# Spreading decay rows by one two-part product, regrouping the key products, and inverting 32x32 blocks on VectorE alone

## The chip, the cores and the metric

The kernel runs on one core of a Trainium2 chip. The metric is device microseconds of the whole launch, the median of several runs of the same program on the same inputs. Five engines of the core work side by side, each through its own instruction queue in order: TensorE (PE; its weight loads are listed as PEld), VectorE (DVE), ScalarE (ACT), GpSimd (POOL) and SyncE (SP), which here issues every DMA. TensorE's clock is granted at one of two levels, 1.2 or 2.4 GHz; the profile gives the granted share of full speed.

## The reference

Two layers of a backbone over 1024 latent tokens and 256 context tokens (1280 together, ten tiles of 128). A layer normalises and modulates its input, projects it by one wide matrix, gives the columns to four groups of four heads each (mLSTM, differential attention, GLA, gated DeltaNet), and brings the four outputs together in an output projection with a gated residual. In the second layer only the latent tokens are put out.

The change lies in the gated DeltaNet. For each direction, each head and each chunk of 64 tokens the reference has:

```
gc = cumsum(g)                                   # along the chunk
decay[t, s] = exp(gc[t] - gc[s])  for s <= t, else 0
lower = (beta k k^T) * decay, strictly below the diagonal
tmat = (I + lower)^-1                            # unit lower triangular, 64x64
u = tmat (v beta),  w = tmat (k beta exp(gc))
attn = (q k^T) * decay
```

A scan over the chunks uses u, w and attn after that. The second direction reads the tokens from the end.

## The kernel before

Two strands of work share the engines. The left one projects: `Proj.run` multiplies the normalised activations by `w_in` block by block (16 blocks a layer; the tiles `mm` of the profile, in two PSUM banks), and then does the mLSTM. The right one goes through a layer in the order `gates`, `gdn`, `attention`, `gla`, and the output projection runs behind them. Layer 1's projections start as layer 0's output rows come in.

The order of the instructions is not written out by hand. All strands hand their next operation to a planner (class `Issue`, from line 131), which keeps a clock per engine from its own cost formulas and takes the operation that can start first, with ranks between strands (`RANK`, line 34: the projections are last with 4, the decays have 1, most of the DeltaNet 0) and with a preference for dense products where its count of streamed columns runs low. What it picks is emitted at once, so its guesses fix each engine's queue; at run time an engine waits at the head of its queue.

The DeltaNet's part before the scan has these steps in each layer:

- `gates` (from line 891) computes rows over all tokens, among them X1 (log decay sum plus log beta) and NCG (minus the decay sum), 8 rows each (direction by head), and writes each by DMA to a DRAM tile of its own, `rs`.
- `gate_columns` (line 1043) reads 8 such tiles back into `pk` (64 rows by 1280 tokens), and PE transposes it to columns `tokc`.
- `gdn_decays` (line 1412) builds exponents as matrices, "column + row": the row has to stand on 32 or 64 partitions. `by_block`, `by_partner` and `by_chunk` do this on PE: the weights are one column of the identity, spread over 32 or 64 columns, the moving side is `pk`, in float32. `by_block` and `by_partner` issue four products of 64x32 weights and 320 columns each, `by_chunk` two of 64x64. There are 28 such units in a layer (8 + 4 + 16), through two PSUM tiles `e`; in the trace a float32 product is two instructions, so they are 160. DVE adds the columns (one operation a unit), POOL adds the mask (16 operations a layer), ACT takes the exponential. The strands `spread` (PE), `exps` (POOL, ACT) and the main one (DVE) hand units over by events.
- `products` in `gdn_rest` (line 1521) multiplies, per tile of 128 tokens and per head, keys by keys in four 32-blocks (64x32 weights) and keys by queries in two 64-chunks (64x64 weights), into `po` and `p1`. Even heads lie on partitions 0 to 63, odd heads on 64 to 127. DVE multiplies the results with the decays into `LT`, `Lo` and `ats`.
- The inverse of every 32x32 diagonal block is by elimination in 31 steps over `Z`: 96 blocks to a partition group are held as three sets of 32x32 on 128 partitions. `steps` (line 1568) does a step as a product into `ltmp` and a subtraction from `Z`. VectorE does sets 0 and 1, each by instructions of its own, GpSimd set 2, in a strand `on_pool`, which at its end clears `T64` for what follows.
- The 64x64 inverses are put together from the blocks by transposes on DVE and 32x32 products on PE; then the scan begins.

In layer 0 the convolution and normalisation of the DeltaNet's inputs (`gdn_front`) and the modulation products (`mod`) run beside the decays; in layer 1 only `gdn_front`.

Of the kernel before, what the change touches and what calls it, by code (L numbers as in the profile page):

```python
# [39 lines left out]
def _consts():  # L40
    f = np.float32
    c = {}
    c["k_zero"] = np.zeros((1, T), f)
    c["k_ident"] = np.eye(128, dtype=f)
    s = np.arange(128)[:, None]
    t = np.arange(128)[None, :]
    c["k_caus"] = np.stack([np.where(t >= s, 0.0, NEG), np.where(t <= s, 0.0, NEG)], 1).astype(f)
    ls = np.arange(128)[:, None] % 32
    lt = np.arange(32)[None, :]
    c["k_m32"] = np.where(lt > ls, 0.0, NEG).astype(f)  # L50
    l6, t6 = np.arange(128)[:, None] % 64, np.arange(64)[None, :]
    c["k_m64"] = np.stack([np.where(t6 >= l6, 0.0, NEG), np.where(t6 <= l6, 0.0, NEG)], 1).astype(f)
    ls = ls.astype(int)
    c["k_lev"] = np.stack([((ls // (2 << j)) == (lt // (2 << j))) & ((ls >> j) != (lt >> j)) for j in range(5)], 1).astype(f)
    bo = np.zeros((128, 128), f)
    bo[:64, :64] = 1
    bo[64:, 64:] = 1
    c["k_bones"] = bo

    sc = np.ones((64, T + 1), f)  # L60
    for r in range(64):
        sc[r, ::128 if r % 32 < 4 else 64] = 0
    c["k_scan"] = sc
    prm = np.zeros((128, 3), f)
    for d in range(2):
        g = 32 * d
        prm[g:g + 4] = (1, 1, 0)
        prm[g + 4:g + 8] = (-1, 0, -1)
        prm[g + 16:g + 32] = (1, 1, 0)
        g = 64 + 32 * d  # L70
        prm[g:g + 4] = (-1, 0, -1)
        prm[g + 4:g + 8] = (1, 0, -1)
    c["k_prm"] = prm
    rows = NLAT // GRID_W
    row = np.repeat(np.arange(rows), GRID_W).astype(f)
    col = np.tile(np.arange(GRID_W), rows).astype(f)
    half = 16
    inv = np.power(f(10000.0), -np.arange(0, half, 2, dtype=f) / f(half)).astype(f)

    def tab(p):  # L80
        ang = (p[:, None] * inv).astype(f)
        ang = np.concatenate([ang, ang], -1)
        return np.cos(ang).astype(f), np.sin(ang).astype(f)

    cr, sr = tab(row)
    cc, scn = tab(col)
    cos = np.concatenate([cr, cc], -1)
    sin = np.concatenate([sr, scn], -1)
    sgn = np.concatenate([-np.ones(8), np.ones(8)] * 2).astype(f)
    cos_all = np.concatenate([np.ones((NCTX, 32), f), cos], 0)  # L90
    sin_all = np.concatenate([np.zeros((NCTX, 32), f), sin * sgn], 0)
    rp = np.stack([cos_all, sin_all], 1)
    c["k_rope"] = rp.reshape(NT, 128, 2, 32).transpose(1, 0, 2, 3).copy()
    return c
# [325 lines left out]
def _build(tc, nc, A, out, root, dbg):  # L420
# [150 lines left out]
    def dt_(name, shape):  # L571
        return dram(shape, name)
# [15 lines left out]
    dod = [dt_(f"do{l}", [128, NT, 256]) for l in L2]  # L588
    dad = [[dt_(f"da{l}_{t}", [128, 8, 64]) for t in range(NT)] for l in L2]
    QN = ("A", "EM", "WS", "NCG", "X1", "EX1", "EX2", "BH", "NG", "WI", "CG", "EG")  # L590
    rsd = [{q: dt_(f"rs{l}_{q}", [8, T]) for q in QN} for l in L2]
    ald = [dt_(f"al{l}", [128, 2, T]) for l in L2]
    AB = [cst([128, 2, 2, 8], f"AB{l}") for l in L2]

# [696 lines left out]
    def gdn(L):  # L1291
        l = L.l
        mark(f"{l}gdn")
        D = Box()
        with ExitStack() as D.st:
            D.ep = Pool(D.st, "gdn", side="right")
            D.st0 = ExitStack()
            D.gp = Pool(D.st0, "gtri", side="right")
            D.LT = D.gp([128, 96, 32], "LT")
            D.Lo = D.gp([128, 40, 32], "Lo")  # L1300
            D.EB = D.ep([128, 5120], "EB")
            D.st1 = ExitStack()
            kp = Pool(D.st1, "keys", side="right")
            D.K = [kp([128, T], f"K{i}") for i in range(2)]
            with ExitStack() as st2:
                D.pk = Pool(st2, "dec", side="right")([64, T], "pk")
                q_.spawn(RANK["decays"], lambda: gdn_decays(L, D, Pool(st2, "dcps", PSUM, "right")))
                for hp in range(2):
                    q_.need((l, "kq", 0, hp))
                    dma(D.K[hp], featd["dkn"][l][:, hp])  # L1310
                q_.need((l, "dec", "e"))
            q_.need((l, "front"))
            kp = Pool(D.st1, "queries", side="right")
            D.Q = [kp([128, T], f"Q{i}") for i in range(2)]
            for hp in range(2):
                q_.need((l, "kq", 1, hp))
                dma(D.Q[hp], featd["dq"][l][:, hp])
            gdn_rest(L, D)
# [93 lines left out]
    def gdn_decays(L, D, pps):  # L1412
# [3 lines left out]
        l = L.l  # L1416
        mark(f"{l}gdn.dec")
        pk, LT, Lo = D.pk, D.LT, D.Lo
        gate_columns(L, pk)
        rows = pk.rearrange("p (t b i) -> p t b i", b=4, i=32)  # L1420
        rows64 = pk.rearrange("p (t c i) -> p t c i", c=2, i=64)
        E2 = D.EB.rearrange("p (l i) -> p l i", i=64)
        first = LT[:, 80:82, :].rearrange("p a b -> p (a b)")[:, :4 * NT].rearrange("p (t h) -> p t h", h=4)
        ib = 8 * QN.index("NCG")
# [4 lines left out]
        def by_block(q, dh):  # L1429

            ps = pps([128, NT, 32], "e", 2)
            for b in range(4):
                r = 8 * QN.index(q) + dh
                P.matmul(ps[32 * b:32 * b + 32], ident[:64, r:r + 1].to_broadcast([64, 32]), rows[:, :, b, :],
                         start=True, stop=True, tile_position=(0, 32 * b))
            return ps

        def by_partner(q, h):

            ps = pps([128, NT, 32], "e", 2)  # L1440
            for b in range(4):
                r = 8 * QN.index(q) + 4 * (b % 2) + h
                P.matmul(ps[32 * b:32 * b + 32], ident[:64, r:r + 1].to_broadcast([64, 32]), rows[:, :, b ^ 1, :],
                         start=True, stop=True, tile_position=(0, 32 * b))
            return ps

        def by_chunk(q, dh, t0):

            r = 8 * QN.index(q) + dh
            ps = pps([128, 5, 64], "e", 2)  # L1450
            for c in range(2):
                P.matmul(ps[64 * c:64 * c + 64], ident[:64, r:r + 1].to_broadcast([64, 64]), rows64[:, t0:t0 + 5, c, :],
                         start=True, stop=True, tile_position=(0, 64 * c))
            return ps

        def tcol(q, dh, n=32, t0=0, m=NT):
# [48 lines left out]
    def gdn_rest(L, D):  # L1505
# [15 lines left out]
        def products():  # L1521
            for t in range(NT):
                if t > 1:
                    q_.need(ev("done", t - 2))

                pk = pks[t] = [pps([128, 2, 128], f"{('po', 'p1')[t % 2]}{x}") for x in range(2)]
                for h in range(4):
                    hp, x = divmod(h, 2)
                    xs = slice(64 * x, 64 * x + 64)
                    for b in range(4):  # L1530
                        t0 = 128 * t + 32 * b
                        both = K[hp][xs, t0 - 32 * (b % 2):t0 - 32 * (b % 2) + 64].rearrange("p (c i) -> p c i", i=32)
                        P.matmul(pk[x][32 * b:32 * b + 32, hp, 0:64].rearrange("p (c i) -> p c i", i=32), K[hp][xs, t0:t0 + 32],
                                 both[:, ::-1] if b % 2 else both, start=True, stop=True, tile_position=(64 * x, 32 * b))
                    for c in range(2):
                        t0 = 128 * t + 64 * c
                        P.matmul(pk[x][64 * c:64 * c + 64, hp, 64:128], K[hp][xs, t0:t0 + 64], Q[hp][xs, t0:t0 + 64],
                                 start=True, stop=True, tile_position=(64 * x, 64 * c))
                q_.set(ev("pk", t))
# [18 lines left out]
        with ExitStack() as st2:  # L1558
# [6 lines left out]
            for s_ in range(3):  # L1565
                V.transpose(Y[:, s_], LT[:, 32 * s_:32 * s_ + 32, :].rearrange("p l t -> p t l"))

            def steps(E, parts):

                for j in range(31):  # L1570
                    m, n = 31 - j, j + 1
                    tv = {}
                    for s_ in parts:
                        tmp = lp([128, 272], f"ltmp{s_}")
                        tv[s_] = tmp[:, :m * n].rearrange("p (a b) -> p a b", b=n)
                        E.tensor_tensor(tv[s_], Y[:, s_, j + 1:, j:j + 1].to_broadcast([128, m, n]),
                                        Z[:, s_, j:j + 1, 0:n].to_broadcast([128, m, n]), ALU.mult)
                    for s_ in parts:
                        E.tensor_tensor(Z[:, s_, j + 1:, 0:n], Z[:, s_, j + 1:, 0:n], tv[s_], ALU.subtract)

            def on_pool():
                mark(f"{l}gdn.inv")
                steps(G, (2,))
                G.memset(T64, 0.0)
                q_.set((l, "inv"))
            q_.spawn(0, on_pool)
            steps(V, (0, 1))
            q_.need((l, "inv"))

            TT, TN = gp([128, 96, 32], "LT"), lp([128, 3, 32, 32], "Y").rearrange("p a b c -> p (a b) c")  # L1590

# [1324 lines left out]
```

## Time and profile before

| | |
|---|---|
| median of three runs | 2483.91 us (2483.13 to 2484.88) |
| the profiled execution | 2481.02 us |
| its span, first to last instruction | 2479.1 us |
| PE busy | 2194.1 us |
| DVE busy | 1521.1 us |
| ACT busy | 980.7 us |
| POOL busy | 905.9 us |
| mean granted TensorE clock | 0.94 |

The span is what the profile's views divide up; the profiled execution's time lies 1.9 us above its span, and the median 2.9 us above that. Busy times are shares of the span of each engine, and they overlap. Nearly all instructions pass through one helper, so they share one source line (L396), and groups are told apart by tile names: `mm` is the projections, `e` the spread rows, `po` and `p` with `K` the key products, `Z` and `ltmp` the inverse.

### The profile page before, as it was taken

Reading aid. Unit: us, or ns where it says so; the run is one execution under the profiler, and the core shown is the slowest. Engines: PE = TensorE matmul, PEld = TensorE weight load, DVE = VectorE, ACT = ScalarE, POOL = GpSimd, SP = SyncE. Lnnn points to the kernel's source line nnn. Section 1 sums busy time; section 2 is a strip of 40 time slices with the busy share of each in tenths; the row PEclk is TensorE's granted clock in tenths of the full one; section 3 lists DMA queues with packets and bytes.
Section 4 is the critical chain, followed back from the end, with each engine's and each line's share of the span. In section 5 each row is a group of like instructions: output and inputs, shape, how many; then the busy total and the mean of one; then the engine's idle time right before and its main releaser. Section 6 shows DMA issues by size and latency. Waiting matters only on the chain. (4 is left out here: it accounts for less than half of the span.)

```text
span 2479.1 us, 58334 instructions
## 1 busy us (share of the span) xinstructions
PE 2194.1 (89%) x23631; PEld 1772.2 (71%) x23631; DVE 1521.1 (61%) x2786; ACT 980.7 (40%) x2123; POOL 905.9 (37%) x1201
## 2 busy tenths in 40 slices
PE   5899999999988998887877899989899898977989
PEld 2666589888776777775755676888778677765777
DVE  3587449664277773447556486587633587746665
ACT  3346211333266773223334265222332476732240
POOL 2233428363212224422431245373533122255340
PEclk7899999999999999998989999999999999976999
DMA  7446442364423215258963244333343422163595
GB/s 258 123 134 226 155 144 92 104 185 143 131 81 99 71 30 149 72 143 229 267 206 115 68 128 144 127 118 101 119 145 108 126 61 67 48 157 97 153 295 182
DMA packets 343414, 334.61 MB, mean 135 GB/s; under 512 B 88762, under 2 KB 287642, under 8 KB 342634
## 3 DMA queue, kind: packets, MB, share of 16 engines
q1 hardware_dynamic: 343146, 330.88, 44.7%
q8 instruction: 187, 3.06, 0.5%
q14 instruction: 81, 0.66, 0.1%
HBM read 225.98 MB, written 107.43 MB: 134 GB/s over the span
## 5 line engine op out<-in xcount | busy, mean ns | idle before, releaser
L396 PE MATMUL mm<-w,hT 128*128 128x256 f32 x4512 | 635.5, 292 | 16.7 <-ACT st L396 5.8
L396 PEld LDWEIGHTS mm<-w,hT 128*128 128x128 f32 x4512 | 571.1, 193 | 58.3 <-issue 31.4
L396 PE MATMUL mm<-hT,w 128*128 128x512 f32 (+1 forms) x1680 | 389.9, 378 | 13.1 <-ACT hT L396 3.7
L396 PEld LDWEIGHTS mm<-hT,w 128*128 128x128 f32 x1680 | 283.1, 194 | 86.0 <-issue 21.2
L396 DVE TENSOR_REDUCE st<-sc 128x1 f32<-128x1024 f32 (+1 forms) x200 | 200.3, 1026 | 85.8 <-PE sc L396 84.4
L396 ACT ACTIVATE p<-sc,st 128x256 f32<-128x256 f32 (+1 forms) x272 | 211.2, 785 | 74.0 <-DVE st L396 55.4
L396 POOL TENSOR_TENSOR hss<-hss,mhalf 128x2 f32<-128x2 f32 (+2 forms) x72 | 103.3, 1435 | 179.0 <-DVE hss L396 171.1
L396 PE MATMUL o<-wo,yT 128*128 128x512 f32 x540 | 151.3, 420 | 5.1 <-DVE x L396 4.8
L396 PE MATMUL sc<-KT,qt 96*128 96x512 f32 (+1 forms) x400 | 123.7, 399 | 31.0 <-DMA KT<-akh 18.4
L396 POOL TENSOR_TENSOR w<-wr,w 128x512 fp32r<-128x512 f32 x60 | 86.3, 1442 | 158.7 <-ACT w L396 120.7
L396 ACT COPY st<-mm 128x512 f32<-128x512 f32 (+1 forms) x84 | 46.1, 549 | 224.1 <-PE mm L396 182.5
L396 POOL TENSOR_TENSOR ss<-ss,mhalf 128x1 f32<-128x1 f32 (+1 forms) x39 | 67.2, 1723 | 183.8 <-DVE ss L396 172.4
L396 POOL TENSOR_TENSOR st<-st 128x1 f32<-128x1 f32 (+1 forms) x136 | 28.0, 206 | 278.1 <-ACT p L396 202.2
L396 ACT COPY wt<-tr 128x512 f32<-128x512 f32 (+1 forms) x200 | 102.3, 511 | 63.8 <-PE tr L396 63.4
L396 PEld LDWEIGHTS o<-wo,yT 128*128 128x128 f32 x540 | 104.8, 200 | 30.0 <-DVE x L396 4.5
L396 PE MATMUL tr<-k_ident,p 128*128 128x128 f32 x656 | 115.1, 281 | 10.1 <-ACT wt L396 9.8
L396 PE MATMUL o<-w,yT 128*128 128x512 f32 x324 | 103.1, 444 | 20.9 <-DVE st L396 15.1
L396 ACT CAST w<-wr 128x512 fp32r<-128x512 f32 x128 | 76.8, 622 | 92.6 <-DMA wr<-in_w_in 58.4
L396 PEld LDWEIGHTS sc<-KT,qt 96*128 96x128 f32 x400 | 63.5, 195 | 59.3 <-ACT p L396 31.8
L396 PE MATMUL po<-wt,av 128*64 128x128 f32 x1312 | 104.6, 284 | 1.4 <-DVE aacc L396 1.4
L396 DVE SCALAR_TENSOR_TENSOR p<-p,st,p 128x1280 f32<-128x1280 f32 (+1 forms) x72 | 103.0, 1431 | 3.1 <-POOL st L396 3.1
L396 PEld LDWEIGHTS tr<-k_ident,p 128*128 128x128 f32 x656 | 75.8, 141 | 36.6 <-ACT wt L396 21.1
(315 smaller groups left out, 4257.3 us busy)
## 6 DMA issues: line engine op xcount, KB each, us to landing
wr<-in_w_in SPq DMA_DIRECT2D x64, 512.0 KB
wm<-in_w_mod SPq DMA_DIRECT2D x64, 256.0 KB
y<-y SPq DMA_DIRECT2D x36, 256.0 KB
xp<-st SPq DMA_DIRECT2D x18, 512.0 KB
pd<-rs_NG SPq DMA_DIRECT2D x18, 512.0 KB
kq<-kq SPq DMA_DIRECT2D x18, 512.0 KB
x<-xp SPq DMA_DIRECT2D x18, 512.0 KB
wm<-in_w_mod SPq DMA_DIRECT2D x16, 512.0 KB
```

The lines of the kernel that those rows point to most:

```text
L396: r = fn(*a, **k)
```

## The change

Three edits. First, the rows are spread by one float32r product a unit with 128x128 weights in place of two or four float32 products. To that end X1 and NCG lie in one DRAM tile; sixteen DMAs and one of a constant bring them to `stage`, arranged so that the 128 partitions are two copies (`part`) of 4 token blocks by 16 rows; ACT rounds `stage` to float32r (`both`, 784 columns), DVE turns the second copy of the rows into what the rounding left over; a 0/1 weight matrix, which ACT spreads out of a 0/1 column for each unit (`adder`), sums the two. The DMAs are issued ahead of those of `gate_columns`. Second, for each tile all heads' K K products are issued before all heads' K Q products. Third, VectorE does all three sets of a step of the inverse in one instruction, and GpSimd only clears `T64` at the last step.

```diff
-    rsd = [{q: dt_(f"rs{l}_{q}", [8, T]) for q in QN} for l in L2]
+    rsd = [{q: dt_(f"rs{l}_{q}", [8, T]) for q in QN if q not in ("X1", "NCG")} for l in L2]
+    rs2 = [dt_(f"rs{l}_X1_NCG", [16, T]) for l in L2]
+    for l in L2:
+        rsd[l].update(X1=rs2[l][0:8], NCG=rs2[l][8:16])
...
+        stage = D.dp([128, 784], "stage")
+        for part in range(2):
+            for b in range(4):
+                dma(stage[64 * part + 16 * b:64 * part + 16 * b + 16, 0:320].rearrange("p (t i) -> p t i", i=32),
+                    rs2[l].rearrange("r (t b i) -> b r t i", b=4, i=32)[b])
+                c, th = divmod(b, 2)
+                dma(stage[64 * part + 16 * b:64 * part + 16 * b + 16, 320:640].rearrange("p (t i) -> p t i", i=64),
+                    rs2[l].rearrange("r (a t c i) -> c a r t i", a=2, c=2, i=64)[c, th])
+        dma(stage[:, 640:784], A["k_pick"])
         gate_columns(L, pk)
-        rows = pk.rearrange("p (t b i) -> p t b i", b=4, i=32)
-        rows64 = pk.rearrange("p (t c i) -> p t c i", c=2, i=64)
+        both = D.dp([128, T], "pk", dt=F32R)
+        S.copy(both[:, 0:784], stage)
+        V.tensor_tensor(both[64:128, 0:640], stage[64:128, 0:640], both[64:128, 0:640].bitcast(F32), ALU.subtract)
...
+        def adder(pick):
+            i, n = turn[0] % 6, pick.shape[1]
+            turn[0] += 1
+            w = spread_[:, 128 * i:128 * i + 128]
+            S.copy(w.rearrange("p (g i) -> p g i", g=n), pick.bitcast(F32).to_broadcast([128, n, 128 // n]))
+            return w
...
             ps = pps([128, NT, 32], "e", 2)
-            for b in range(4):
-                r = 8 * QN.index(q) + dh
-                P.matmul(ps[32 * b:32 * b + 32], ident[:64, r:r + 1].to_broadcast([64, 32]), rows[:, :, b, :],
-                         start=True, stop=True, tile_position=(0, 32 * b))
+            r = 8 * ("X1", "NCG").index(q) + dh
+            P.matmul(ps, adder(pick_b[:, :, r:r + 1]), blocks, start=True, stop=True)
             return ps
...
                                  both[:, ::-1] if b % 2 else both, start=True, stop=True, tile_position=(64 * x, 32 * b))
+                for h in range(4):
+                    hp, x = divmod(h, 2)
+                    xs = slice(64 * x, 64 * x + 64)
                     for c in range(2):
                         t0 = 128 * t + 64 * c
                         P.matmul(pk[x][64 * c:64 * c + 64, hp, 64:128], K[hp][xs, t0:t0 + 64], Q[hp][xs, t0:t0 + 64],
...
-            q_.spawn(0, on_pool)
-            steps(V, (0, 1))
-            q_.need((l, "inv"))
+            for j in range(31):
+                m, n = 31 - j, j + 1
+                if j == 30:
+                    G.memset(T64, 0.0)
+                tmp = lp([128, 3 * 272], "ltmp")
+                tv = tmp[:, :3 * m * n].rearrange("p (s a b) -> p s a b", s=3, b=n)
+                V.tensor_tensor(tv, Y[:, :, j + 1:, j:j + 1].to_broadcast([128, 3, m, n]),
+                                Z[:, :, j:j + 1, 0:n].to_broadcast([128, 3, m, n]), ALU.mult)
+                V.tensor_tensor(Z[:, :, j + 1:, 0:n], Z[:, :, j + 1:, 0:n], tv, ALU.subtract)
```

`by_partner` and `by_chunk` are changed as `by_block` is. The new constant `k_pick` (128x144) holds the three sets of 0/1 columns.

## Rows read from the trace of the kernel before

**Rows 1.** The page's first part: busy us (share of the span) xinstructions, by engine.
```profile
PE 2194.1 (89%) x23631; PEld 1772.2 (71%) x23631; DVE 1521.1 (61%) x2786; ACT 980.7 (40%) x2123; POOL 905.9 (37%) x1201
```

**Rows 2.** Who waited for whom, PE, 62 to 1057 us: total us, times, longest.
```profile
PE sc L396 <- DMA KT<-akh: 9.6, 2, 5.7
```

**Rows 3.** Chain of waits, end of layer 1: start us, us, what.
```profile
2175.68 11.64 PE mm L396 x96
...
2188.74 8.21 DMA gk<-gqk
```

**Rows 4.** Busy time by stretch: length, engines (xinstructions), PEclk, DMA share, GB/s.
```profile
235.00:306.00 71.00, 68.82 (x467) 35.49 (x467) 34.22 (x53) 22.95 (x39) 28.36 (x28) 0.98 0.46 147
368.00:444.00 76.00, 71.98 (x541) 68.14 (x541) 68.38 (x151) 14.72 (x26) 53.31 (x74) 0.98 0.30 96
1495.00:1566.00 71.00, 67.09 (x483) 46.79 (x482) 49.06 (x52) 34.80 (x53) 42.76 (x35) 0.95 0.32 107
1632.00:1712.00 80.00, 71.57 (x457) 66.38 (x458) 62.22 (x149) 14.52 (x26) 53.95 (x74) 0.91 0.29 94
2170.00:2232.00 62.00, 43.45 (x1056) 40.81 (x1054) 29.69 (x61) 20.06 (x38) 31.53 (x43) 0.76 0.62 156
2232.00:2294.00 62.00, 45.61 (x1510) 36.34 (x1510) 40.31 (x53) 18.73 (x39) 31.71 (x39) 0.69 0.38 96
```

**Rows 5.** The same for the tile `e` alone: PE, PEld, DVE, then the clock.
```profile
235.00:306.00 71.00, 25.20 (x160) 6.34 (x160) 13.29 (x28) 0.98 0.46 147
1495.00:1566.00 71.00, 20.89 (x160) 5.81 (x160) 13.16 (x28) 0.95 0.32 107
```

**Rows 6.** The same for the tile `K` alone, the key products: PE, PEld.
```profile
300.00:357.00 57.00, 21.42 (x480) 13.96 (x480) 1.00 0.46 151
1566.00:1620.00 54.00, 21.77 (x480) 14.31 (x480) 1.00 0.48 157
```

**Rows 7.** Timeline of PE in one tile's key products: start us, us, instructions.
```profile
310.04 0.33 PE L396 MATMUL po<-Q,K 64*64 64x64 f32 x4
310.30 0.32 PE L396 MATMUL po<-K 64*32 64x64 f32 x8
310.55 0.33 PE L396 MATMUL po<-Q,K 64*64 64x64 f32 x4
```

**Rows 8.** Busy time for the tile `Z` alone, the inverse: PE, PEld, DVE, ACT, POOL.
```profile
368.00:444.00 76.00, 0.00 (x0) 0.00 (x0) 52.79 (x123) 0.00 (x0) 37.16 (x62) 0.98 0.30 96
1632.00:1712.00 80.00, 0.00 (x0) 0.00 (x0) 48.02 (x125) 0.00 (x0) 36.18 (x61) 0.91 0.29 94
```

**Rows 9.** Timeline of DVE in layer 0's inverse.
```profile
400.29 1.54 DVE L396 TENSOR_TENSOR ltmp<-Y,Z 128x231 f32<-128x231 f32 x2
...
418.89 0.75 DVE L396 TENSOR_TENSOR ltmp<-Y,Z 128x256 f32<-128x256 f32 x2
419.56 0.75 DVE L396 TENSOR_TENSOR Z<-Z,ltmp 128x256 f32<-128x256 f32 x2
...
443.75 0.31 DVE L396 TENSOR_TENSOR ltmp<-Y,Z 128x31 f32<-128x31 f32 x2
```

**Rows 10.** Who waited for whom, DVE, 1632 to 1712 us.
```profile
DVE w L396 <- ACT w L396: 9.3, 3, 5.2
DVE st L396 <- ACT th L396: 6.3, 3, 4.6
```

**Rows 11.** The page's third part: DMA packets, MB, share of 16 engines' span.
```profile
q1 hardware_dynamic: 343146, 330.88, 44.7%
```

**Rows 12.** Timeline of SP's DMA issues, and PE's first `e` in layer 1.
```profile
1482.41 0.32 SPq L396 DMA_DIRECT2D pk<-rs_A  x1
...
1503.00 1.43 PE L396 MATMUL e<-pk,k_ident 64*32 64x320 f32 x12
...
2178.12 8.61 SPq L396 DMA_DIRECT2D gv<-gv  x4
```

**Rows 13.** The tile `ot`: ns min/median/max, first and last start.
```profile
L396 ACT COPY ot<-po x36: 265/316/327, 703.0 to 2171.5; 128x128 f32<-128x128 f32 x36
```

More of the change, by code (lines that the diff above doesn't have):

```diff
@@ L63, in _consts @@
     c["k_scan"] = sc
+    p, r = np.arange(128)[:, None, None], np.arange(16)[None, None, :]
+    g = np.arange(4)[None, :, None]
+    by_block = (p // 16 % 4 == g) & (p % 16 == r)
+    th, cc = np.arange(2)[None, :, None, None], np.arange(2)[None, None, None, :]
+    p4, r4 = p[..., None], r.reshape(1, 1, 16, 1)
+    by_chunk = (p4 // 32 % 2 == cc) & (p4 // 16 % 2 == th) & (p4 % 16 == r4)
+    h, g = np.arange(4)[None, :, None], np.arange(4)[None, None, :]
+    by_partner = (p // 16 % 4 == (g ^ 1)) & (p % 16 == 4 * (g % 2) + h)
+    c["k_pick"] = np.concatenate([x.reshape(128, -1) for x in (by_block, by_chunk, by_partner)], 1).astype(f)
     prm = np.zeros((128, 3), f)
@@ L1305, in gdn @@
             with ExitStack() as st2:
-                D.pk = Pool(st2, "dec", side="right")([64, T], "pk")
+                D.dp = Pool(st2, "dec", side="right")
+                D.pk = D.dp([128, T], "pk")[0:64]
                 q_.spawn(RANK["decays"], lambda: gdn_decays(L, D, Pool(st2, "dcps", PSUM, "right")))
@@ L1418, in gdn_decays @@
         pk, LT, Lo = D.pk, D.LT, D.Lo
-        gate_columns(L, pk)
-        rows = pk.rearrange("p (t b i) -> p t b i", b=4, i=32)
-        rows64 = pk.rearrange("p (t c i) -> p t c i", c=2, i=64)
+        stage = D.dp([128, 784], "stage")
[7 more added lines that the diff above has]
+        dma(stage[:, 640:784], A["k_pick"])
+        gate_columns(L, pk)
+        both = D.dp([128, T], "pk", dt=F32R)
+        S.copy(both[:, 0:784], stage)
+        V.tensor_tensor(both[64:128, 0:640], stage[64:128, 0:640], both[64:128, 0:640].bitcast(F32), ALU.subtract)
+        blocks, chunks = both[:, 0:320], both[:, 320:640]
+        pick_b = both[:, 640:704].rearrange("p (g r) -> p g r", g=4)
+        pick_c = both[:, 704:768].rearrange("p (a r c) -> p a r c", a=2, c=2)
+        pick_p = both[:, 768:784].rearrange("p (h g) -> p h g", h=4)
+        spread_ = D.dp([128, 784], "stage", dt=F32R)
+        turn = [0]
+        def adder(pick):
[4 more added lines that the diff above has]
+            return w
         E2 = D.EB.rearrange("p (l i) -> p l i", i=64)
@@ L1440, in by_partner @@
             ps = pps([128, NT, 32], "e", 2)
[L1441 to L1444, printed above, removed]
+            P.matmul(ps, adder(pick_p[:, h, :].unsqueeze(2)), blocks, start=True, stop=True)
             return ps
         def by_chunk(q, dh, t0):
-            r = 8 * QN.index(q) + dh
+            r = 8 * ("X1", "NCG").index(q) + dh
             ps = pps([128, 5, 64], "e", 2)
-            for c in range(2):
-                P.matmul(ps[64 * c:64 * c + 64], ident[:64, r:r + 1].to_broadcast([64, 64]), rows64[:, t0:t0 + 5, c, :],
-                         start=True, stop=True, tile_position=(0, 64 * c))
+            P.matmul(ps, adder(pick_c[:, t0 // 5, r, :].unsqueeze(2)), chunks, start=True, stop=True)
             return ps
@@ L1566, in gdn_rest @@
                 V.transpose(Y[:, s_], LT[:, 32 * s_:32 * s_ + 32, :].rearrange("p l t -> p t l"))
[L1568 to L1585, printed above, removed]
-            q_.spawn(0, on_pool)
-            steps(V, (0, 1))
-            q_.need((l, "inv"))
+            for j in range(31):
[7 more added lines that the diff above has]
+                V.tensor_tensor(Z[:, :, j + 1:, 0:n], Z[:, :, j + 1:, 0:n], tv, ALU.subtract)
             TT, TN = gp([128, 96, 32], "LT"), lp([128, 3, 32, 32], "Y").rearrange("p a b c -> p (a b) c")
```

## The prediction

> **What bounds the kernel now.** I read the engine totals first. PE is busy 2194.1 of 2479.1 us, DVE 1521.1, the others less [rows 1]: PE is the nearest to a bound, but a mean over stages proves nothing. So I took the waits of PE from 62 to 1057 us, where layer 0's projections run. The longest entry is 9.6 us in almost a thousand [rows 2]. PE hardly stands there: whenever the DeltaNet strand waits for something, the planner puts projections in its place. The stretches show the same: 68.82 of 71 us busy in the decays of layer 0, 71.98 of 76 in its inverse, 67.09 of 71 and 71.57 of 80 in layer 1 [rows 4]. It follows that in these stages a microsecond of PE work removed is worth about a microsecond, and that a shorter inverse is worth little by itself: the projections that stood beside it have to be done later.
>
> The exception is the end of layer 1. The chain of waits goes through the last 96 projection products (11.64 us) and then through a DMA of the GLA (8.21 us) [rows 3], so there the DeltaNet-attention-GLA strand comes late while the projections run out. From 2170 to 2294 us PE is busy only 43.45 and 45.61 of 62 us, at a granted clock of 0.76 and 0.69, a mixture of both levels [rows 4]. If the strand is ahead of the projections there, some of the 34.9 us of idle PE are filled.
>
> **The change part by part.** All sums are made against the profiled execution, 2481.0 us; the median lies 2.9 us higher, and I add that at the end.
>
> *Spread rows, PE.* Before, the tile `e` takes 25.20 and 20.89 us of PE in the two layers, 160 instructions each [rows 5], 46.1 us together. After, 28 products a layer, each 128x128 weights against 320 float32r columns. The nearest rows are the projections, which are float32r with full weights too: 96 products of 256 columns in 11.64 us [rows 3], 0.121 us each, so 0.152 us for 320 columns, 4.3 us a layer, 8.5 us in all. Removed: 46.1 - 8.5 = 37.6 us. If the rounding of weights and rows made a product cost twice that, 29.1 us would be left; more than 46.1 can't be gained.
>
> *Spread rows, the new wait.* Each product now waits for its weights, a copy on ACT, 56 in all. The nearest row is a copy of 128x128 on ACT, 0.316 us [rows 13], so 17.7 us of ACT, which is busy 22.95 and 34.80 of 71 us there [rows 4]: room enough. But queues are in order. Behind a product that waits, projections and transposes stand on PE; behind a late ACT instruction, the copy. Nothing in the trace shows this wait. At best it costs nothing (PE is the later engine, its weights are ready); at worst each product waits for one other ACT instruction of about a microsecond, 56 us. In the stage before, PE idles only 2.2 and 3.9 us [rows 4], so PE is the late one; I take 0.15 us each, 8 us.
>
> *Staging.* Sixteen DMAs and one for the constant are put into SP's queue ahead of the eight of `pk`, and the DMAs queued after them on SP (convolution rows, weights, stores) move back too. At 0.32 us an issue [rows 12] that is 5.4 us. They are 8 x 160 + 8 x 80 = 1920 pieces of 128 or 256 bytes; a packet takes 44.7% x 16 x 2479.1 / 343146 = 0.052 us of one DMA engine on average [rows 11], so 6.2 us for 1920 on sixteen free ones. In layer 1, `pk` is issued at 1482.4 and the first spread starts at 1503.0 [rows 12], 20 us with room in them. Then come a cast of 784 columns on ACT and a subtraction on DVE, about 0.9 us each by the price of an element worked out below [rows 9]. The delay is 0 to 12 us a layer for the DeltaNet strand, during which PE has projections to do. I charge 3 us in all. The masks, column sums and exponentials stay.
>
> The DMA issue of `gv`, also in 256-byte pieces, held SP 8.61 us for four instructions of 1280 pieces [rows 12], 2.2 us each where 0.32 is usual. The Trainium skill ("DMA: Bandwidth & Descriptors", Specifications) states that transfers under 512 B do not reach line rate. By that and this row, 1920 pieces would hold SP 3.2 us beyond the plain pieces' share and land later; the sum would lose some 3 us more.
>
> *Key products.* K takes 21.42 and 21.77 us of PE [rows 6], in groups that start 0.26 and 0.25 us after one another and alternate in weight shape [rows 7]. Eight instructions of 64 columns, at the projections' 0.121 us for 256, are 0.24 us: no room for a switch there; four are 0.12 us, which leaves 0.13 us at each pair. Of the eight alternations a tile six go. Between 0 and 6 x 10 x 2 x 0.13 = 16 us are gained; I take half, 8 us.
>
> Before, even and odd heads (two halves of the rows) never overlap: each group starts when the former is through [rows 7]. The Trainium skill ("TensorEngine Tiling (Array Packing)", Tiling Modes) has different row tiles run in parallel when the mode stays the same. No row here shows it; the rival below prices it.
>
> *Inverse.* DVE's share is now 52.79 and 48.02 us for two sets, POOL's 37.16 and 36.18 us for one [rows 8], in stretches of 76 and 80 us. Two DVE operations of 256 elements start 0.67 us apart in quiet moments, 0.335 us each; from 0.75 us for two of 256 and 0.31 for two of 31, an element costs 0.00098 us, and the fixed part is 0.085 us [rows 9]. All three sets are 62 instructions with 2 x 3 x 5456 = 32736 elements: 5.3 + 32.1 = 37 us. The other DVE work of the stretch is 68.38 - 52.79 = 15.6 us, in layer 1 14.2 us [rows 4, 8]. While POOL works, DVE's operations take up to twice as long (1.54 us for two of 231 elements [rows 9]); POOL keeps 53.31 - 37.16 = 16 us of other work, for which I add 8 us. So 37 + 15.6 + 8 = 61 us instead of 76. In layer 1 DVE also stands for casts and evacuations that come late, 9.3 and 6.3 us [rows 10]; with 10 us of that, 69 instead of 80. Bounds: 53 us with no contention, 37 x 2 + 16 = 90 us with POOL beside it all along. PE is full of projections under it, so what comes back is PE's idle time in proportion: 4.0 x 15/76 + 8.4 x 11/80 = 2 us.
>
> *The end of layer 1.* The strand is some 11 us further ahead than the projections. Of the 34.9 us idle it fills between 0 and 20; I take 8 us.
>
> Sum: -37.6 + 8 + 3 - 8 - 2 - 8 = -44.6 us. 2481.0 - 44.6 + 2.9 = 2439 us.
>
> **The rivals.** *PE's saving turns into waits (2469 us).* If another engine sets the pace of the decays, PE only idles more. DVE's 34.22 and 49.06 of 71 us there [rows 4] leave room, which speaks against it; that the strands hand on through two PSUM tiles in strict turns speaks for it. Half of 37.6 us and nothing else, with the staging: -18.8 + 3, 2468 us.
>
> *The row halves overlap (2425 us).* Then the key products shrink to half, 43.2 to 21.6 us [rows 6], 13.6 us more than I took. For it: the halves are independent and write different tiles. Against: no group overlaps now.
>
> *The strand decides throughout (2394 us).* If the projections always have room, the inverse's 26 us and some 10 us in the decays count in full, with 16 us of the products: -37.6 - 16 - 26 - 10, the two charges falling away, 2394 us. The full PE of rows 4 speaks against it.
>
> *Slower (2495 us).* Place: PE's queue in the decays. A product stands for its weights on ACT, and the projections behind it stand with it. If ACT runs behind the plan by 1.1 us at each of the 56, that costs 62 us, against 52 gained elsewhere: 2481 + 2.9 + 62 - 52, 2494 us. It decides from about 0.9 us a product. For it: in the decays of layer 1 ACT is at 34.80 of 71 us, its operations come in bursts, and the planner's clock, not the chip's, orders the queues. Against: PE is the late engine now.
>
> *Nothing to be seen (2484 us).* The new order of the planner may lose elsewhere what is gained; no row speaks for it, but every queue after the decays is ordered anew.
>
> **How the numbers follow.** Chances: the forecast 0.53 (its own range 2420 to 2460), row halves 0.07, PE's saving lost 0.18, the strand throughout 0.07, nothing 0.06, slower 0.09. A measurement can tell about 0.2%, 5 us, from no change. Faster: 0.53 + 0.07 + 0.18 + 0.07 make 0.85; same 0.06; slower 0.09. For 8 in 10 the range goes down to 2402, which takes in half the gap to 2394, and up to 2482, which takes in the half-lost case and its spread but not the slower one.
>
> **What would show it.** In the profile after: `e` at about 4 us of PE a layer in 28 products; idle of PE in front of `e` for ACT under 10 us; `K` near 17 us a layer; the inverse at 61 and 69 us with POOL nearly free; the last `mm` of layer 0 about 20 us earlier than 1057; more than 46 us of PE busy in each half of the stretch after attention in layer 1. The prediction is wrong if PE's busy time falls by 45 us and the span doesn't, or if the inverse lasts longer than before.

## The result and the profile after

The kernel after takes 2444.24 us (median of 4 runs, 2441.89 to 2447.24), the kernel before on the same chip 2483.52 us (4 runs). The ratio is 0.9845, with a 95% interval of 0.9821 to 0.9869: 39 us faster, 5 us above the predicted 2439 and well inside its range. The profiled execution took 2444.9 us, its span is 2443.0 us. The total was right; the experiments show that the way to it was right only in part.

The page's first part for the kernel after, which answers to [rows 1]:

```profile
span 2443.0 us, 57689 instructions
PE 2141.1 (88%) x23367; PEld 1762.3 (72%) x23367; DVE 1513.1 (62%) x2676; ACT 987.4 (40%) x2169; POOL 850.4 (35%) x1075
```

PE lost 2194.1 - 2141.1 = 53.0 us of work, and its idle time rose from 285.0 to 301.9 us; the difference is the span's 36.1 us. The tiles `e` (first two lines) and `K` (last two) account for nearly all of the work that went, [rows 5, 6]:

```profile
255.00:292.00 37.00, 8.92 (x28) 4.96 (x28) 13.11 (x28) 1.00 0.54 172
1520.00:1560.00 40.00, 9.68 (x28) 5.44 (x28) 13.17 (x28) 0.96 0.42 127
...
296.00:336.00 40.00, 9.61 (x480) 6.71 (x480) 1.00 0.64 217
1560.00:1600.00 40.00, 10.28 (x480) 7.23 (x480) 0.96 0.52 178
```

`e` fell from 46.1 to 18.6 us, `K` from 43.2 to 19.9. How the key products got so short is seen in PE's timeline of one tile, beside [rows 7]:

```profile
326.66 0.45 PE L406 MATMUL po<-K 64*32 64x64 f32 x32
327.05 0.46 PE L406 MATMUL po<-Q,K 64*64 64x64 f32 x16
327.44 0.45 PE L406 MATMUL p<-K 64*32 64x64 f32 x32
```

From start to start, the 32 instructions of K K take 0.39 us and the 16 of K Q as long, 0.78 us together, where a tile took 43.2 / 20 = 2.16 before. The starts of the single instructions in both traces show two causes.

First, PE starts nothing for a while at each change of the weight shape. In the kernel before, the key products come in 162 groups of one shape, and after 161 of them the next instruction, of another shape, starts 0.145 to 0.149 us after the group's last. In the kernel after there are 44 groups. 118 x 0.147 = 17 us of the 23.3 is thus an estimate for the regrouping alone.

Second, products on different blocks of the array start 0.007 us apart and run beside each other. A window that ends 0.05 us behind the first start of K K has these instructions, first before, then after:

```profile
310.30 0.26 PE L396 MATMUL po<-K 64*32 64x64 f32 x4
...
302.61 0.29 PE L406 MATMUL p<-K 64*32 64x64 f32 x8
```

Before, the four column blocks of one head already ran so; after, the four of the other half of the rows follow at once. A product's second instruction starts 0.080 us after its first in both kernels (for K Q 0.107 in both), though after, the other half's instructions have started in between. So the two halves of the rows do run beside each other, in both shapes, which the forecast gave a chance of 0.07. The Trainium skill ("TensorEngine Tiling (Array Packing)", Tiling Modes) has different row tiles run in parallel while the mode stays the same: the trace now agrees.

The inverse on DVE alone (tile `Z`), beside [rows 8]:

```profile
344.00:407.00 63.00, 0.00 (x0) 0.00 (x0) 47.95 (x63) 0.00 (x0) 0.00 (x0) 1.00 0.32 101
1609.00:1675.00 66.00, 0.00 (x0) 0.00 (x0) 45.60 (x63) 0.00 (x0) 0.00 (x0) 0.95 0.29 92
```

It lasts 63 and 66 us instead of 76 and 80. The staging shows on SP's queue, where before the first `pk` was issued at 219.42 us:

```profile
219.69 4.38 SPq L406 DMA_DIRECT2D stage<-rs_X_NCG  x7
225.56 0.36 SPq L406 DMA_DIRECT2D wm<-in_w_mod  x1
225.96 1.67 SPq L406 DMA_DIRECT2D stage<-rs_X_NCG  x3
...
238.82 0.29 SPq L406 DMA_DIRECT2D pk<-rs_A  x1
```

`pk` goes out 19.4 us later, and the first `e` starts at 259.9 instead of 241.2 us, in layer 1 at 1524.9 instead of 1503.0 [rows 12]. But the planner has set the staging between other loads (`wm` is a weight load of the modulation), and PE hardly waits: 3.0 us in all in front of `e` for its weights (0.4 and 2.6 us in the two layers).

Where the lead comes and goes is read from the same instructions in PE's timeline of both kernels, first before, then after: the first `m` of the mLSTM in layer 0, the projection of layer 1 that waits for the last `hT`, the first `m` of layer 1.

```profile
1071.06 0.66 PE L396 MATMUL m<-k_ident,kq 128*128 128x128 f32 x2 [4.44 <-DMA kq<-kq]
1367.32 0.80 PE L396 MATMUL mm<-hT,w 128*128 128x512 f32 x1 [3.01 <-ACT hT L396]
2234.16 0.69 PE L396 MATMUL m<-k_ident,kq 128*128 128x128 f32 x2 [3.08 <-DMA kq<-kq]
```

```profile
1069.60 0.69 PE L406 MATMUL m<-k_ident,kq 128*128 128x128 f32 x2 [7.22 <-DMA kq<-kq]
1362.33 0.79 PE L406 MATMUL mm<-hT,w 128*128 128x512 f32 x1 [3.01 <-ACT hT L406]
2197.66 0.69 PE L406 MATMUL m<-k_ident,kq 128*128 128x128 f32 x2 [0.22 <-DMA kq<-kq]
```

In layer 0 the inverse ends 38 us earlier (406 instead of 444), the last projection 17 us (1040.2 instead of 1056.9), but the mLSTM starts only 1.5 us earlier: it stands 7.22 us for its load, where it stood 4.44. The very first projections of layer 1 start at 1283.43 instead of 1295.28 us, but at the one shown the lead is 5.0 us, and from there 31.5 us more come up to layer 1's mLSTM. The forecast had counted the layers alike.

### The profile page after: what moved, and what is told of

Its sections match the earlier page's. It is cut to its first block, busy times and chain, and to the rows that moved or that the text cites. A ratio compares the mean times of both kernels' runs of the same rounds, so it can differ in the third digit from the quotient of the medians.

```text
span 2443.0 us, 57689 instructions
## 1 busy us (share of the span) xinstructions
PE 2141.1 (88%) x23367; PEld 1762.3 (72%) x23367; DVE 1513.1 (62%) x2676; ACT 987.4 (40%) x2169; POOL 850.4 (35%) x1075
## 4 chain that ended last, share of the span: by engine, by line
PE 55%; DMA 13%; DVE 11%; issue 8%; ACT 6%; SPq 5%; POOL 2%; ACTq 0%; POOLq 0%; DVEq 0%
PE mm L406 26%; PE po L406 5%; SPq L406 5%; PE tr L406 4%; PE o L406 4%; PE sc L406 3%; PE p L406 3%; PE pd L406 3%; DVE st L406 2%; DMA wm<-in_w_mod 2%; PE puw L406 2%; ACT p L406 2%; PE m L406 2%; DVE cacc L406 1%; DMA KT<-akh 1%
## 5 line engine op out<-in xcount | busy, mean ns | idle before, releaser
L406 PE MATMUL mm<-w,hT 128*128 128x256 f32 x4512 | 645.6, 294 | 20.7 <-DVE st L406 10.0
L406 PEld LDWEIGHTS mm<-w,hT 128*128 128x128 f32 x4512 | 580.9, 195 | 52.9 <-issue 20.4
L406 PEld LDWEIGHTS o<-wo,yT 128*128 128x128 f32 x540 | 105.7, 202 | 34.7 <-issue 5.6
L406 DVE TENSOR_TENSOR w<-wr,w 128x512 fp32r<-128x512 f32 x66 | 59.1, 895 | 68.6 <-ACT w L406 64.9
```

The source lines that it names most:

```text
L406: r = fn(*a, **k)
```

## The experiments

Theory A is the forecast's: PE is the bound, so a microsecond of PE removed is worth one in either layer. Theory B: what counts is how early the DeltaNet strand is in layer 1, since layer 0's tail swallows its lead. Theory C, set up after the first four of these runs: what a part is worth hangs on the order that the planner makes of everything behind it. All ratios are against the kernel before on the same chip; the rows come from four chips, so differences between rows are taken from the ratios.

| kernel | ratio (95%) | median us |
|---|---|---|
| decays alone | 1.0016 (0.9998-1.0035) | 2489.5 |
| product order alone | 1.0001 (0.9985-1.0016) | 2486.8 |
| inverse alone | 1.0095 (1.0077-1.0112) | 2507.9 |
| decays and product order | 0.9944 (0.9923-0.9965) | 2471.6 |
| all, layer 0 only | 0.9987 (0.9970-1.0005) | 2484.3 |
| all, layer 1 only | 0.9941 (0.9915-0.9968) | 2470.8 |
| before, planner's margin 0.17 | 1.0144 (1.0102-1.0186) | 2523.1 |
| after, planner's margin 0.17 | 0.9910 (0.9889-0.9932) | 2463.9 |
| product order, queues kept | 0.9946 (0.9925-0.9967) | 2475.7 |
| inverse, queues kept | 0.9998 (0.9981-1.0015) | 2486.9 |
| all, queues kept | 1.0012 (0.9992-1.0033) | 2488.8 |
| all, queues kept, half the staging | 0.9965 (0.9944-0.9986) | 2475.7 |

**One part at a time, planned anew.** Each is the kernel before with one part of the change as it stands in the diff above.

```diff
 # decays alone
+            P.matmul(ps, adder(pick_b[:, :, r:r + 1]), blocks, start=True, stop=True)
 # product order alone
+                for h in range(4):
+                    hp, x = divmod(h, 2)
 # inverse alone
+                V.tensor_tensor(Z[:, :, j + 1:, 0:n], Z[:, :, j + 1:, 0:n], tv, ALU.subtract)
```

> Only the decays are changed (spread by one product, with its staging); products and inverse as before. Theory A (the forecast's: PE is the bound, a microsecond of PE removed is worth one in either layer): e falls by 27 to 37 us of PE, less the charges for weights and staging, 22 to 32 us faster, so about 2457. Theory B (what counts is how early the DeltaNet strand is in layer 1; in layer 0 the stretch after the projections swallows the lead): in the trace after the change the decays of layer 1 end at 1556.3 us instead of 1555.7, since the staging gives back what the products save; so 0 to 8 us faster, about 2480.

> Only the order of the key products is changed. Tile K should fall from 43.2 to about 20 us of PE, as in the trace after the change (if it stays near 35, the overlap of the row halves came from something else). Theory A: 20 to 24 us faster, about 2461. Theory B: only layer 1's share counts, 10 to 13 us faster, about 2472.

> Only the inverse is changed (all three sets on VectorE). The stage should last 61 to 66 us instead of 76 and 80. Theory A: PE is full beside it, so 2 to 4 us faster, about 2481. Theory B: the strand of layer 1 comes 14 us earlier and this counts, 10 to 14 us faster, about 2471.

Measured: +4, 0 and +24 us. The inverse alone fits neither A nor B: it is shorter (layer 0's ends at 429 instead of 444), and still the kernel loses 24 us. The decays alone are near B's number; the product order alone gained nothing, which neither A nor B had. Added up, the three come to +28 us; together they give -39. The parts do not add.

**Two parts together.**

```diff
 # the hunks of the decays and of the product order; the inverse keeps
             q_.spawn(0, on_pool)
             steps(V, (0, 1))
```

> Decays and product order as after, inverse as before. Each of the two alone brought nothing, the inverse alone 24 us slower. Theory A: about 5 us slower than the whole change, 2449. Theory B: the strand of layer 1 lacks the inverse's 14 us, so 2458. Theory C: 2440 to 2500.

Measured 14 us faster, 25 us behind the whole change: worse than A and B allow. So the inverse, which loses 24 us alone, brings 25 to these two.

**One layer at a time.** The same kernel with all three parts in one layer only.

```diff
+                q_.spawn(RANK["decays"], lambda: (gdn_decays if l == 0 else gdn_decays_old)(L, D, Pool(st2, "dcps", PSUM, "right")))
...
+                if l == 0:
...
+            if l == 0:
```

> All three parts in layer 0 only; layer 1 as before. Theory A: half of the 39 us, 17 to 22 us faster, about 2464. Theory B: the lead of layer 0 is lost behind its projections, 3 to 7 us faster, about 2479.

> All three parts in layer 1 only; layer 0 as before. Layer 0 alone brought 0.1%, the whole change 1.55%. Theory B (the strand of layer 1 decides): 33 to 38 us faster, about 2449. Theory A (PE saved counts one for one): 17 to 22 us, about 2464. Theory C (what a part is worth hangs on the order in which the planner puts projections and strand afterwards, and scatters by 10 to 25 us): no number follows; 2440 to 2500.

Layer 0 gives 3 us (not told apart from nothing), layer 1 15 us, the sum 18 and not 39. That layer 0 alone is worth little is as B has it, and as the trace of the kernel after shows at 1071 and 1367 us; but B's 33 to 38 us for layer 1 were missed. A's 17 to 22 were missed for layer 0; for layer 1 their lower part lies inside the interval, 8 to 21 us.

**Nothing changed but the order.** The planner adds a margin ahead of each PE instruction; from the DeltaNet of layer 0 on, it is made a little larger.

```diff
         mark(f"{l}gdn")
+        q_.MARGIN = 0.17
         D = Box()
```

> The kernel before with one number of the planner changed from the DeltaNet of layer 0 on (the margin that it adds ahead of a PE instruction, 0.15 to 0.17 us): the same instructions in another order. Theories A and B: nothing is removed and the strand isn't earlier, so within 5 us of before. Theory C: 10 to 25 us away from before, more likely slower.

> The kernel after with the same number changed at the same place. Theories A and B: within 5 us of 2444. Theory C: 10 to 25 us away from 2444, more likely slower; if both this and the kernel before with the new number move alike, the difference between them still is the change's.

The kernel before lost 36 us by it, the kernel after 16. The same instructions in another order (up to a few copies that the planner gives to another engine) differ by nearly as much as the whole change gains, so A and B fall as accounts of the single kernels above. With the larger margin the change is worth 59 us (2523.1 to 2463.9), with the old one 39: that it helps holds in both.

**The parts with the queues kept.** To price a part without a new order, the planner is told of the old instructions and the new ones are put into their places: every other instruction keeps its place in its engine's queue. For the products 48 old places take 48 new instructions; for the inverse the second of VectorE's two operations does all three sets, and the first and POOL's are left empty.

```diff
 # product order, queues kept
+                for (a, k), (a2, k2) in zip(old, kk + kq):
+                    q_("P", "matmul", lambda *_, a=a2, k=k2, **__: P.raw.matmul(*a, **k), a, k)
 # inverse, queues kept
+                        if E is V and s_ == 1:
+                            return V.raw.tensor_tensor(Z[:, :, j + 1:, 0:n], Z[:, :, j + 1:, 0:n], all_, ALU.subtract)
 # decays, queues kept (with the two above: all)
+                if i == n - 1:
+                    return P.raw.matmul(ps, on["w"], rows_, start=True, stop=True)
+            q_("P", "matmul", emit, a, k)
```

> The key products in their new order, put into the places that the old ones had: every other instruction of every engine keeps its place in its queue (the planner is told of the old products). Tile K should fall from 43 to about 20 us of PE. The forecast's premise (in these stages PE is full, so a microsecond of it is worth one): 18 to 23 us faster, about 2464. If what the parts bring comes only from the planner's new order: within 5 us of before.

> The inverse on VectorE alone, every other instruction in its old place. The forecast's step: PE is full beside it, so 2 us faster, between 0 and 6, about 2482; the 24 us that the inverse alone lost were then the new order's. If the inverse on VectorE itself holds up what else VectorE does there (casts, evacuations): 10 to 24 us slower.

> All three parts in the order of before. The forecast's sum without the end of layer 1: -37.6 + 8 + 3 - 8 - 2, with the products at the -23 measured instead of -8: about 50 us faster, 2433. But the order of before has the spread start at 241 and 1503 us, and the staging lands some 20 us later: if the products of the spread hold PE's queue for it, up to 20 us a layer come back, 2433 to 2473. If the gain of the whole change is one of the new order: within 10 us of before.

The product order alone is 13 us faster, the interval being 8 to 19 us. Tile `K` of that run, in both layers:

```profile
300.00:360.00 60.00, 11.72 (x480) 7.86 (x480) 0.97 0.51 165
1560.00:1625.00 65.00, 13.40 (x480) 9.11 (x480) 0.92 0.46 148
```

43.2 - 25.1 = 18.1 us of PE are gone, and 13 come through in time. That is the cleanest support for the forecast's rate of exchange (its profiled execution, 2480.9 us, was the slowest of its six, so its trace can't place the gain; PE's busy time as a whole is 9.8 us less there, at a granted clock of 0.935 instead of 0.940). The run of the inverse changed nothing in time, but it hardly tests what a shorter inverse is worth: in layer 0 the inverse didn't get shorter (it ended at 447.5 instead of 444.1 us), in layer 1 by 4 of 81 us. VectorE's other work stands between its steps where it stood before, and in layer 0 that waits for ACT (11.6 us in three pieces):

```profile
DVE w L396 <- ACT w L396: 11.6, 3, 9.4
```

All three together gain nothing, 3 us slower. Its page has PE at 2158.9 us, 35 less than before; the idle time is 43 us more. PE's waits in 215 to 310 us (two lines) and in 1475 to 1575 us (two lines) say for what:

```profile
PE mod L406 <- DMA wm<-in_w_mod: 13.9, 4, 13.0
PE e L1467 <- ACT stage L1464: 7.2, 5, 3.9
...
PE tr L406 <- DMA raw<-dqr: 11.8, 1, 11.8
PE e L1467 <- ACT stage L1464: 9.3, 5, 4.4
```

The columns are total, times, longest. 13.0 and 11.8 us in one piece are for loads that have nothing to do with the decays: a weight of the modulation and a convolution row. SP's queue shows why; here are the first and the last of the 17 staging issues and the load behind them:

```profile
216.72 0.64 SPq L1440 DMA_DIRECT2D stage<-rs_X_NCG  x1
217.41 0.59 SPq L1443 DMA_DIRECT2D stage<-rs_X_NCG  x1
...
226.67 0.43 SPq L1445 DMA_DIRECT2D stage<-in_k_pick  x1
...
233.93 0.36 SPq L406 DMA_DIRECT2D wm<-in_w_mod  x1
```

The 17 issues hold the queue for 10.4 us, and `wm`, issued at 224.50 us before, goes out at 233.93. In the kernel before, PE stood 1.4 and 1.6 us in all for the same two loads. Another 16.5 us stand in front of `e` for its weights on ACT.

**Half the staging.** The lower 64 partitions alone are loaded, and VectorE writes the low parts into the upper ones.

```diff
-        for part in range(2):
-            for b in range(4):
+        for b in range(4):
...
-        V.raw.tensor_tensor(both[64:128, 0:640], stage[64:128, 0:640], both[64:128, 0:640].bitcast(F32), ALU.subtract)
+        V.raw.tensor_tensor(both[64:128, 0:640], stage[0:64, 0:640], both[0:64, 0:640].bitcast(F32), ALU.subtract)
```

> All three parts in the order of before, as in the run before, but with half the staging: the 8 DMAs for the upper 64 partitions are left out, and VectorE writes the low parts there from the lower half. In the run before, 17 issues held the SP queue from 216.7 to 227.1 us; PE then stood 13.0 us in one piece for a weight load of the modulation queued behind them, and 11.8 us in layer 1 for a convolution row. Theory S (the place in the SP queue takes the gain): some 5 us less in each of the two waits, 8 to 12 us faster than 2489, about 2479, ratio about 0.996. Rival (another engine sets the pace of the spread, and PE's idle only changes its name): the two waits may shrink, but the spread still ends at 307 and 1572 us and the time stays within 4 us of 2489.

The ratio is 0.9965, as theory S had it: 12 us faster than with the whole staging. The same waits, in the same two stretches:

```profile
PE mod L406 <- DMA wm<-in_w_mod: 8.2, 4, 7.1
PE e L1467 <- ACT stage L1464: 7.1, 5, 3.8
...
PE e L1467 <- ACT stage L1464: 8.9, 5, 4.3
PE tr L406 <- DMA raw<-dqr: 6.8, 1, 6.8
```

The longest pieces fell by 5.9 and 5.0 us, 10.9 together; the waits for ACT did not move. The spread ends at 302.8 and 1558.7 instead of 307.1 and 1572.4 us. That the staging in front of these loads took this part of the gain is thereby shown, for the order kept; the run takes out issues and bytes together, so it doesn't tell the queue from the transfers. No version beat the kernel after.

## Why the prediction was right, and where it was not

- **The total.** 44.6 us were forecast against the profiled 2481.0, 36.1 came. The forecast's case is the nearest of all, but its sum holds by errors that cancel: more PE work went than was forecast, and idle time and a lower clock, which it hardly charged, took the difference back (table below).
- **The premise, that a microsecond of PE removed is worth one.** It holds in part. With every queue kept as it was, the products alone pass on 13 of 18 us; with all three parts PE does 35 us less and the kernel is no faster. There PE stands 39 us longer than before for the two loads behind the staging and for the weights (13.9 + 11.8 + 7.2 + 9.3 against 1.4 + 1.6), against the 11 charged: these charges failed, and the rate of exchange is not refuted by it. It takes the planner's new order, in which other work closes up, to turn the removed work into time: in 235 to 310 us of the kernel after PE is busy 71.91 of 75 us, with the queues kept 63.58. "PE's saving turns into waits" (0.18) is what all parts together did in the old order, but not for its reason: the waits are for loads and weights, not for another engine that sets the pace.
- **Spread rows, PE.** Forecast -37.6, measured -27.5 by tile `e`. A product starts 0.15 us before the next instruction in a full stream (266.49 to 266.64 us), as worked out; the tile's busy time counts 0.32 us for each, with the overlap. With the decays alone, PE's work as a whole is 39 us less at full speed (table below), near the forecast.
- **The wait for weights.** Forecast +8. In the kernel after it is 3.0 us, with the queues kept 16.5: it depends on the order. The slower rival's price, 1.1 us a product, wasn't reached in either.
- **Staging.** Forecast +3 of PE and 0 to 12 us of delay for the strand; measured 18.7 and 22 us of delay. An issue was priced at 0.32 us [rows 12], 5.4 us for 17; they took 10.4. The sentence that the DMAs behind them move back too was written down, and not priced: in the old order it costs 24.8 us of PE in two waits. By the row of `gv` the issues would have come to 5.4 + 3.2 = 8.6 us, nearer than mine, but also without the loads behind.
- **Key products.** Forecast -8 of at most 16, measured -23.3 of PE, worth 13 us of time with the queues kept. The price of a change of shape was read too low: 0.13 us for a pair of changes, since eight instructions of K K were taken one after another, 0.24 us. Four of them start within 0.02 us, and each of the two changes costs 0.15 us. The overlap of the halves was left to a rival.
- **Inverse.** Forecast 61 and 69 us, measured 63 and 66. What the shorter inverse is worth in the old order no run shows. The price of an element was taken at 418.89 us as a quiet moment; GpSimd was at work there too, but in a memset. That the inverse brings 25 us where decays and products have been changed, and costs 24 where they haven't, is of the size that the order alone moves, and no term of the sum had that.
- **End of layer 1.** Forecast -8 by a strand ahead there, more than 46 us of PE in each half of the stretch after attention. In the 124 us from 2120 it is busy 54.32 and 40.28 us, 94.6 instead of 89.1 [rows 4]: 5.5 us, and one half fell short.
- **The layers.** Forecast alike; layer 0 alone gives 3 us, layer 1 alone 15.

A term that the sum lacked is the granted clock. Each trace records when which level was granted, so PE's busy time can be split by level: before, 219.1 us of it lie at the lower level, with the margin of 0.17 281.9 us. If busy time at the lower level is counted half, PE's work is 2084.5 and 2086.1 us, the same, as it should be for the same products. So the difference of a profiled execution to the one before splits into three parts, in us and rounded:

| kernel | PE's work at full speed | lower clock | PE idle | span |
|---|---|---|---|---|
| after | -62 | +9 | +17 | -36 |
| decays alone | -39 | +15 | +28 | +4 |
| product order alone | -18 | +8 | +21 | +12 |
| before, planner's margin 0.17 | +2 | +31 | +16 | +49 |
| product order, queues kept | -19 | +9 | +10 | 0 |
| all, queues kept | -53 | +18 | +43 | +8 |

The parts alone did take PE's work away, the decays about as much as was forecast and the products more; what hid it is idle time and a lower clock. This says where the time went in these executions, not what in the order brings it about.

Open is what makes one order 16 to 36 us better than another. The kernel with the inverse alone has its last projections of layer 0 at 1079 instead of 1057 us, and from 1040 to 1370 us PE stands 34.7 us for the DMA of `y`, where before it stood 12.0; what in the order decides it was not found. One other order for each kernel is too few to say how much of the 39 us is the change and how much the luck of this order: 39 in one pair, 59 in the other. The products with the halves of the rows kept apart, which would separate the overlap from the alternations by a run, were not tried; the split above rests on the starts in the traces.

## What to carry to other kernels

Where a planner or a scheduler orders the queues anew, measure a change also with the queues kept, and the unchanged kernel in another order: only then is it known what is the change and what is the order, and parts tested singly need not add up. When PE's busy time is compared, split it by the granted clock first. Of small DMAs put ahead of others, price the loads queued behind them first, those of other stages above all; the engine stands there and not at the consumer. A stretch where an engine is busy 97% tells that its work is worth time only if something is ready to take the place.

## What was not expected of the hardware

- In the kernel before, 0.145 to 0.149 us lie from the last start of a group of key products to the next instruction, whichever other shape that has; on different blocks of the array, in one shape, starts lie 0.007 us apart. So 32 instructions of 64 columns start within 0.24 us, and of the time of products as small as these the changes of shape are a large part.
- A staging issue of 160 pieces of 128 bytes held SP 0.54 to 0.64 us, one of 80 pieces of 256 bytes 0.58 to 0.59 (but for one of 0.31): more than the 0.32 us of a plain one, and not by the number of pieces. `gv`'s 1280 pieces took 2.2 us each [rows 12].
- Where PE stood for the two loads, the granted clock fell with it. Busy time and clock from 215 to 310 and 1475 to 1575 us, with the queues kept and all three parts; before, the two stretches had 91.37 and 91.70 us of PE at 0.98 and 0.97:

```profile
215.00:310.00 95.00, 72.86 (x442) 50.12 (x440) 48.76 (x70) 42.25 (x84) 36.53 (x36) 0.86 0.52 164
1475.00:1575.00 100.00, 73.55 (x426) 62.65 (x425) 59.65 (x61) 52.54 (x94) 43.65 (x41) 0.85 0.41 132
```

  Part of those stretches ran at the lower level, 1.2 instead of 2.4 GHz, so that part of the work left was done more slowly; over the whole execution the mean was 0.929, before 0.940.
